# One stick-breaking pass in three steps instead of four, a small product issued later, and 70 column-square additions given to GpSimd

## The chip, the cores and the metric

The kernel runs on one core of a Trainium2 chip. A core has five engines that work at the same time, each through its own queue of instructions in a fixed order: TensorE (PE, matrix products, with its weight loads shown apart as PEld), VectorE (DVE), ScalarE (ACT), GpSimd (POOL) and SyncE (SP, which here issues transfers). They share an on-chip memory of 128 partitions. A tile of "128x512" has one row of 512 elements on each partition. An instruction that needs another engine's result waits on a semaphore, and everything behind it in the same queue waits with it.

The metric is the device time of one execution in microseconds (us). Smaller is better.

## The reference

One inference step of a two-layer decoder with D = 1024. A prompt of 1024 tokens and 8 sample tokens pass through the same weights. Cut to what matters here:

```python
def rmsnorm(x, g):
    return x * lax.rsqrt(jnp.mean(x * x, axis=-1, keepdims=True) + EPS) * g

# layer 0: HGRN2 recurrence beside attention into 256 memory tokens, then a SwiGLU FFN
# then one shared K/V is projected from the residual stream
# layer 1: stick-breaking attention over the shared K/V beside memory attention, then an FFN
h = h + rmsnorm(mix, g[1])
h = h + rmsnorm(swiglu(rmsnorm(h, g[2]), w_gu, w_down), g[3])

def stick_breaking(q, k, v, bias, ...):          # blocks of 128 queries, 4 heads
    z = q @ k.T * scale + bias
    mask = k_pos < q_pos
    log_keep = where(mask, log_sigmoid(-z), 0)
    tail = cumsum(log_keep, reverse=True) - log_keep
    w = where(mask, exp(log_sigmoid(z) + tail), 0)
    return w @ v
```

The outputs are the residual streams of prompt and sample, the recurrence states, the shared K/V and the memory K/V.

## The kernel before, in words

**Tiling.** The prompt is cut in two groups of 512 tokens, g = 0 and g = 1; group 1 carries the 8 sample tokens as well, so its tiles are 520 columns wide. Activations lie with features on the partitions, eight tiles of 128 features for D = 1024. Every f32 weight tile is split into a high and a low part, the high part by a cast on ACT (line 217 or 618), the low part by a subtraction on DVE (line 218 or 620); a product then takes three matmuls per weight tile (high times high, high times low, low times high). Lines 231, 551, 625 and 797 are those matmuls, so PE often waits, when it waits, for a weight part `ws`. A part of each FFN is computed by a scheme with fewer products (`ffn_w`, `gate_up_w`), which adds up blocks of weights first (lines 605 to 612 on DVE). Sums of weights that are used often are made ahead of time by GpSimd's accumulating transfers, "weight sums" (lines 695 to 700).

**Order of the work.** The kernel is written as Python generators. `weave` advances several of them in turn by given weights, `drain` runs one to its end. The order in which instructions are written, data dependencies and the number of buffers in each pool (four tiles `c`, seven tiles `b`, two tiles `n`) feed a scheduler that fixes each engine's queue. So a change in one generator can move instructions of its neighbours.

**Column squares.** The RMS norm needs, for every token, the sum of squares over 1024 features. `sq_acc` (lines 284 to 290) is called for eight feature tiles: the first square goes into the accumulator `st`; each of the other seven goes into a tile `n` on ACT (line 289), and DVE adds it to the accumulator (line 290). `rstd_from` then splits the accumulator in a high part (cast on ACT, line 238) and a low part (subtraction on DVE, line 239), sums over the partitions with two matmuls against ones (line 279), and takes logarithm and exponential on ACT (lines 280 and 281). The results scale the next projection's input.

**Token scales.** At the very start, `token_scales` computes the first norm's scale per token; a diagonal tile (line 363) is multiplied with ones on PE (line 368) so that every partition has all 512 scales, and ACT copies them to `rows`. `gate_proj` multiplies by them.

**Stick-breaking, group 0.** `sb_prompt` runs four heads with three units each (the blocks of queries 0 and 2 together, block 1, block 3). `weights` makes a unit's scores on PE (line 1609), adds bias and mask on DVE (lines 1620 and 1622), takes two ACT passes for softplus into a tile `e` (lines 1595 and 1596), scans on DVE (line 1632), subtracts (line 1634) and exponentiates on ACT (line 1635). `turn` transposes the result on PE (line 1641) and copies it on ACT (line 1643), `values` multiplies by the values on PE (line 1652). `step` shifts units through `asked`, `scored` and `turned`: a unit's scores are made in one step, the transposes come two steps later, the values one step after that, and three empty steps at the end flush the rest. The tile `e` is half of a `c` tile; the FFN's weight blocks (the operands `c` of lines 605 to 620) are in `c` tiles too. This pass is woven with memory attention on one side and with parts 0 and 1 of the other group's FFN on the other.

Of the kernel before, what the change touches and what calls it, by code (L numbers as in the profile page):

```python
# [23 lines left out]
def tile_decoder(  # L24
# [96 lines left out]
    def S():  # L121
        return smp.tile([P, 512], F32, tag="s", name=nm("s"))
# [149 lines left out]
    def rstd_from(acc, n, inv, dst=None, bank=NS):  # L272
# [8 lines left out]
        nc.scalar.activation(r[:, :n], r[:, :n], AF.Exp, scale=-0.5)  # L281
        return r

    def sq_acc(acc, src, k, n):
        if k == 0:
            nc.scalar.activation(acc[:, :n], src, AF.Square)
        else:
            t = N()
            nc.scalar.activation(t[:, :n], src, AF.Square)  # L289
            nc.vector.tensor_add(acc[:, :n], acc[:, :n], t[:, :n])  # L290

    def normed(g, R, rstd, gc, out, keep=False):
        n = NG[g]
# [56 lines left out]
    def token_scales(out):  # L350
        ss = small([P, 8], tag="rr")
        for tb in range(CH):
            xt = xtok[0][:, tb, :]
            junk = M().rearrange("p a n -> p (a n)")[:, :D]
            with tc.issue_after(turned[-1][tb % 2]):
                if tb % 2:
                    nc.vector.tensor_tensor_reduce(junk, xt, xt, 1.0, 0.0, ALU.mult, ALU.add, ss[:, tb : tb + 1])
                else:
                    nc.scalar.activation(junk, xt, AF.Square, accum_out=ss[:, tb : tb + 1])
        nc.scalar.activation(ss[:, :CH], ss[:, :CH], AF.Ln, scale=1.0 / D, bias=epsb)  # L360
        nc.scalar.activation(ss[:, :CH], ss[:, :CH], AF.Exp, scale=-0.5)
        d = B()
        nc.vector.tensor_mul(
            d.rearrange("p (c t) -> p c t", c=CH), ident.unsqueeze(1).to_broadcast([P, CH, P]),
            ss[:, :CH].unsqueeze(2).to_broadcast([P, CH, P]),
        )
        ps = S()
        nc.tensor.matmul(ps, ones, d, start=True, stop=True)
        rows = M()[:, 0, :G]
        nc.scalar.copy(rows, ps)  # L370
        out.extend((ss, rows))

    def start(g, out):
        if g:
# [900 lines left out]
                nc.vector.tensor_copy(vs[:, h, :], t[:, G : G + NB])  # L1275
            yield

    def gate_proj(g, W, xt, Ft, Kt, rows):
        n = NG[g]
        for h in range(H):  # L1280
            if h % 2 == 0:
                Ft.append(A())
                Kt.append(A())
            ps = proj(g, W, 0, ND, 4 * P + h * P, xt)
            f = T()
            if rows is None:
                nc.scalar.copy(sv(f, g), pv(ps, g))
            else:
                nc.vector.tensor_mul(sv(f, g), pv(ps, g), rows)
            e = T()  # L1290
            nc.vector.scalar_tensor_tensor(e[:, :n], f[:, :n], -1.0, f[:, :n], op0=ALU.mult, op1=ALU.min)
            nc.scalar.activation(e[:, :n], e[:, :n], AF.Exp)
            nc.scalar.activation(e[:, :n], e[:, :n], AF.Ln, bias=1.0)
            nc.vector.scalar_tensor_tensor(e[:, :n], f[:, :n], 0.0, e[:, :n], op0=ALU.min, op1=ALU.subtract)
            nc.vector.tensor_sub(f[:, :n], e[:, :n], f[:, :n])
            Fd = Ft[-1][:, h % 2, :n]
            Kd = Kt[-1][:, h % 2, :n]
            nc.scalar.activation(Fd, e[:, :n], AF.Exp)
# [188 lines left out]
    class mixer_a:  # L1487
# [7 lines left out]
            return lambda dst, ps, g: evac(dst, ps, g, self.scales[1])  # L1495

        def fq(self):
            yield from gate_proj(self.g, self.W, self.xt, self.F, self.K, self.scales[1])
            yield from heads2(self.g, self.W, 0, self.xt, self.scaled(silu), A, self.Q)

        def v(self):
# [96 lines left out]
    def sb_prompt(g, Qs, xo):  # L1598
# [5 lines left out]
        def weights(h, kh, unit, first):  # L1604
            ps, spans, o = S(), [], 0
            for c, s in unit:
                w = (c + 1) * P if s == g else G
                spans.append((c, s, o, w))
                nc.tensor.matmul(  # L1609
                    ps[:, o : o + w], Qs[h // 2][:, h % 2, c * P : (c + 1) * P], kh[:, s, :w], start=True, stop=True  # L1610
                )
                o += w
            zb = B()
            bh, i = biasp[:, h : h + 1], 0
            for c, s, a, w in spans:
                if s != g:
                    continue
                j = a + w - P
                if i < j:
                    nc.vector.tensor_scalar(zb[:, i:j], ps[:, i:j], bh, 44.0, op0=ALU.add, op1=ALU.min)  # L1620
                i = j + P
                nc.vector.scalar_tensor_tensor(zb[:, j:i], ps[:, j:i], bh, cap, op0=ALU.add, op1=ALU.min)
            if i < o:
                nc.vector.tensor_scalar(zb[:, i:o], ps[:, i:o], bh, 44.0, op0=ALU.add, op1=ALU.min)
            if not spare:
                c = C()
                spare.extend((c[:, 0], c[:, 1]))
            e = spare.pop(0)
            softplus(zb, e, o)
            for c, s, a, w in spans:  # L1630
                d = e[:, a : a + w][:, ::-1]
                nc.vector.tensor_tensor_scan(d, d, d, first.get(c, 0.0), op0=ALU.add, op1=ALU.max)
                first[c] = e[:, a : a + 1]
            nc.vector.tensor_sub(zb[:, :o], zb[:, :o], e[:, :o])
            nc.scalar.activation(zb[:, :o], zb[:, :o], AF.Exp)  # L1635
            return zb, spans, o
# [26 lines left out]
        def step(new=None):  # L1663
            nonlocal asked, scored, turned
            old, turned = turned, asked and (*asked[0], *turn(*asked[1]))
            asked, scored = scored, new
            if old:
                values(*old)

        for h in range(H):  # L1670
# [4 lines left out]
            for i, unit in enumerate(units):  # L1675
                step(((h, vh, i), weights(h, kh, unit, first)))
                yield
        for _ in range(3):
            step()
            yield  # L1680

# [178 lines left out]
        f0.acc = fw.acc  # L1860

    weave((chain(a1.merge(), a1.mem()), 36), (ms, 74), (rest(), 33))
    xk0, xb0 = [], []
    o1 = out_proj(1, 0, M)
    drain(o1.mm(a1.xo, 0, 1, True))
# [7 lines left out]
    b0.open(True)  # L1873
    set_banks(True)
    fw = ffn_w(1, 0, o1.x, (5, 6, 5), 0, False, beside=(0, 1), src=o1.R)
    weave((chain(b0.sb(), b0.mem()), 26), (chain(fw.part(0), fw.part(1)), 28))
    p4 = fw.part(4)
    back = b0.load()
    drain(fw.part(2), islice(back, 4))
    weave((chain(fw.part(3), islice(p4, 8)), 20), (weight_sums(1, (4,)), 16))  # L1880
    weave((p4, 4), (back, 8))
    f1 = ffn(1, 0, o1.x)
    f1.R, f1.acc = fw.R, fw.acc
# [63 lines left out]
```

## Time and profile before

| | |
|---|---|
| median of 3 runs | 2404.77 us (2404.55 to 2404.97) |
| the profiled execution | 2404.09 us |
| its span, first to last instruction | 2402.4 us |
| granted TensorE clock, mean | 0.998 |
| PE busy | 2379.4 us, 99% of the span |
| DVE busy | 1711.9 us, 71% |
| ACT busy | 1323.8 us, 55% |
| POOL busy | 113.0 us, 5% |

Lines of a view by time have a start in microseconds from the span's start, a duration, the engine, the line, the operation and the tiles (output <- inputs). Rows that follow each other closely are joined: x96 is 96 instructions, and the duration is that of all of them. A bracket at the end is the idle time of the engine just ahead of the row, and what ended it. Rows of windows give the window, its length, then for PE, PEld, DVE, ACT and POOL the busy time (and number of instructions), then the granted clock as a share of full speed, the share of DMA engines busy, and GB/s.

### The profile page before, as it was taken

The numbers are of one execution on the slowest core, as the hardware profiler recorded it, in microseconds if no ns is written. First come the engines' busy times: TensorE is split into PE (matmuls) and PEld (weight loads), VectorE is DVE, ScalarE is ACT, GpSimd is POOL, SyncE is SP. The second block draws the span as 40 slices with busy tenths as digits, with TensorE's granted clock in tenths as the row PEclk, the third lists the DMA queues.
The fourth block names the chain that finished last, engine by engine and source line by source line (L and its number), as shares of the span: only waits on it lengthen the run. The fifth ranks groups of instructions, "written<-read, shape, count | busy, mean of one in ns | idle before, by whom it ended". The sixth has DMA issues, their size and how long they took to land.

```text
span 2402.4 us, 42455 instructions
## 1 busy us (share of the span) xinstructions
PE 2379.4 (99%) x15962; PEld 2159.8 (90%) x15962; DVE 1711.9 (71%) x3197; ACT 1323.8 (55%) x2734; POOL 113.0 (5%) x187
## 2 busy tenths in 40 slices
PE   8999999999999999999999999999999999999998
PEld 7888989888889998899999989887778989999998
DVE  5867558766776676778665777876776779676866
ACT  4547544454664554566544554568547566554545
POOL 1001202101000000000001100112000000000000
PEclk9999999999999999999999999999999999999999
DMA  6354776677535446332668746544454354343442
GB/s 195 118 171 115 174 203 159 166 188 197 169 105 164 140 146 203 104 119 90 170 177 219 212 143 189 167 144 149 121 174 123 96 156 128 118 127 100 115 124 76
DMA packets 515231, 357.58 MB, mean 149 GB/s; under 512 B 20245, under 2 KB 463746, under 8 KB 515026
## 3 DMA queue, kind: packets, MB, share of 16 engines
q1 hardware_dynamic: 499154, 312.93, 43.9%
q0 software_dynamic: 15872, 41.95, 7.5%
q8 instruction: 125, 2.05, 0.4%
q14 instruction: 80, 0.66, 0.1%
HBM read 322.86 MB, written 65.49 MB: 162 GB/s over the span
## 4 chain that ended last, share of the span: by engine, by line
PE 93%; DVE 3%; ACT 2%; DMA 1%; issue 1%; SPq 0%; DVEq 0%; ACTq 0%
PE mm L231 42%; PE q L625 18%; PE q L797 12%; PE q L551 4%; PE mm L1250 2%; PE s L1429 1%; PE s L1609 1%; PE s L1652 1%; PE s L1066 1%; PE s L1047 1%; PE mm L983 1%; PE mm L1010 1%; PE q L829 1%; PE s L551 1%; PE s L1641 1%
## 5 line engine op out<-in xcount | busy, mean ns | idle before, releaser
L231 PE MATMUL mm<-x,ws 128*128 128x512 f32 (+1 forms) x5016 | 924.1, 342 | 3.7 <-ACT b L1635 1.7
L231 PEld LDWEIGHTS mm<-x,ws 128*128 128x128 f32 x5016 | 775.1, 188 | 114.5 <-ACT b L1635 2.1
L217 ACT CAST ws<-w 128x512 fp32r<-128x512 f32 x596 | 346.0, 584 | 392.9 <-PE mm L231 229.2
L218 DVE TENSOR_TENSOR ws<-w,ws 128x512 fp32r<-128x512 f32 x596 | 380.3, 645 | 222.5 <-ACT ws L217 219.0
L797 PE MATMUL q<-m,ws 128*128 128x260 f32 (+1 forms) x2496 | 304.6, 283 | 1.6 <-ACT m L238 1.0
L797 PEld LDWEIGHTS q<-m,ws 128*128 128x128 f32 x2496 | 300.1, 188 | 3.1 <-ACT m L238 1.6
L625 PE MATMUL q<-y,ws 128*128 128x260 f32 (+1 forms) x1920 | 251.0, 285 | 0.0
L625 PEld LDWEIGHTS q<-y,ws 128*128 128x128 f32 x1920 | 238.4, 189 | 2.2 <-DVE ws L620 0.7
L625 PE MATMUL q<-x,ws 128*128 128x260 f32 (+1 forms) x1668 | 220.0, 283 | 3.5 <-DVE ws L620 1.7
L625 PEld LDWEIGHTS q<-x,ws 128*128 128x128 f32 x1668 | 207.9, 189 | 4.3 <-DVE ws L620 2.1
L231 PE MATMUL mm<-m,ws 128*128 128x512 f32 x768 | 186.9, 397 | 0.0
L618 ACT CAST ws<-w 128x512 fp32r<-128x512 f32 x206 | 124.9, 619 | 97.6 <-PE q L797 30.8
L231 PEld LDWEIGHTS mm<-m,ws 128*128 128x128 f32 x768 | 142.7, 188 | 31.9
L620 DVE TENSOR_TENSOR ws<-w,ws 128x512 fp32r<-128x512 f32 x206 | 139.3, 688 | 43.6 <-ACT ws L618 40.7
L806 DVE TENSOR_TENSOR r<-r,q 128x260 f32<-128x260 f32 (+1 forms) x160 | 60.6, 420 | 49.0 <-PE q L797 48.2
L551 PE MATMUL q<-x,ws 128*128 128x260 f32 (+1 forms) x720 | 87.1, 282 | 0.0
L551 PEld LDWEIGHTS q<-x,ws 128*128 128x128 f32 x720 | 86.4, 188 | 0.3
L238 ACT CAST m<-t 128x512 fp32r<-128x512 f32 (+1 forms) x88 | 54.6, 621 | 40.3 <-DVE t L870 16.9
L618 ACT CAST ws<-b 128x512 fp32r<-128x512 f32 x82 | 50.6, 620 | 42.3 <-PE q L797 13.4
L239 DVE TENSOR_TENSOR m<-t,m 128x512 fp32r<-128x512 f32 (+1 forms) x88 | 60.8, 691 | 14.7 <-ACT m L238 13.9
L620 DVE TENSOR_TENSOR ws<-b,ws 128x512 fp32r<-128x512 f32 x82 | 56.4, 688 | 19.3 <-ACT ws L618 18.9
L290 DVE TENSOR_TENSOR st<-st,n 128x512 f32<-128x512 f32 (+1 forms) x91 | 62.3, 692 | 3.4 <-ACT n L289 1.9
(427 smaller groups left out, 3119.3 us busy)
## 6 DMA issues: line engine op xcount, KB each, us to landing
w<-in_w_gu SPq DMA_DIRECT2D x275, 256.0 KB
w<-in_w_down SPq DMA_DIRECT2D x160, 256.0 KB
wsum<-in_w_gu POOLq DMA_DIRECT2D x48, 512.0 KB, 6.6
w<-in_w_in_a SPq DMA_DIRECT2D x80, 256.0 KB
w<-in_w_o SPq DMA_DIRECT2D x64, 256.0 KB
w<-wsum SPq DMA_DIRECT2D x61, 256.0 KB
b<-in_w_gu SPq DMA_DIRECT2D x39, 256.0 KB
b<-wsum SPq DMA_DIRECT2D x39, 256.0 KB
```

The costliest lines, as they stand in the source:

```text
L217: nc.scalar.copy(ws[:, 0, :n, :], raw[:, :n, :])
L218: split[0] = nc.vector.tensor_sub(ws[:, 1, :n, :], raw[:, :n, :], ws[:, 0, :n, :].bitcast(F32))
L231: nc.tensor.matmul(ps[:, a, : PW[g]], wt, xt[k][:, xi, o : o + PW[g]], start=(k == 0 and wi == 0), stop=(k == nk - 1 and wi == 2),)
L238: nc.scalar.copy(dst[0], src)
L239: nc.vector.tensor_sub(dst[1], src, dst[0].bitcast(F32))
L290: nc.vector.tensor_add(acc[:, :n], acc[:, :n], t[:, :n])
L551: ins = nc.tensor.matmul(pp[a][:, :h], wt, xt[k][:, xi, a * h : (a + 1) * h], start=(k == 0 and wi == 0), stop=(k == ND - 1 and wi == 2),)
L618: nc.scalar.copy(w[:, 0, :], src)
L620: split[0] = nc.vector.tensor_sub(w[:, 1, :], src, w[:, 0, :].bitcast(F32))
L625: nc.tensor.matmul(ps[:, :h], w[:, wj, k * P : (k + 1) * P], x[:, xi, :], start=(first and k == 0 and wi == 0), stop=(k == 3 and wi == 2), ...
L797: nc.tensor.matmul(pp[a][:, :h], wt, mids[k][:, xi, a * h : (a + 1) * h], start=(k == 0 and wi == 0), stop=(k == nf - 1 and wi == 2),)
L806: nc.vector.tensor_add(d, d, pp[a][:, :h])
```

## The change

There are three edits. **A**: a flag `free` sends line 290's additions to GpSimd while it is set. It is set ahead of layer 0's last output projection, is taken back for the one stretch in which weight sums are being made, and is set again after that. By the order of the changed program 70 of the 91 additions move, as ten sums of seven; the remaining 21 stay on DVE. **B**: the ones product of the token scales moves from `token_scales` to a function that `gate_proj` calls at its first head. **C**: in stick-breaking of group 0, `step` passes a new unit straight on, so that the transposes come one step after the scores instead of two; two empty steps flush instead of three; `e` comes from the pool of `b` tiles; the weight in `weave` is 25 instead of 26.

```diff
+    free = [False]
     def sq_acc(acc, src, k, n):
...
-            nc.vector.tensor_add(acc[:, :n], acc[:, :n], t[:, :n])
+            (nc.gpsimd if free[0] else nc.vector).tensor_add(acc[:, :n], acc[:, :n], t[:, :n])
...
+        out.extend((ss, d))
+
+    def scale_rows(scales):
         ps = S()
-        nc.tensor.matmul(ps, ones, d, start=True, stop=True)
+        nc.tensor.matmul(ps, ones, scales[1], start=True, stop=True)
         rows = M()[:, 0, :G]
         nc.scalar.copy(rows, ps)
-        out.extend((ss, rows))
+        scales[1] = rows
...
-                nc.vector.tensor_mul(sv(f, g), pv(ps, g), rows)
+                if h == 0:
+                    scale_rows(scales)
+                nc.vector.tensor_mul(sv(f, g), pv(ps, g), scales[1])
...
-            if not spare:
+            if g and not spare:
                 c = C()
                 spare.extend((c[:, 0], c[:, 1]))
-            e = spare.pop(0)
+            e = spare.pop(0) if g else B()
...
-            asked, scored = scored, new
+            asked, scored = (scored, new) if g else (new, None)
...
-        for _ in range(3):
+        for _ in range(2 + g):
...
     weave((chain(a1.merge(), a1.mem()), 36), (ms, 74), (rest(), 33))
+    free[0] = True
...
-    weave((chain(b0.sb(), b0.mem()), 26), (chain(fw.part(0), fw.part(1)), 28))
+    weave((chain(b0.sb(), b0.mem()), 25), (chain(fw.part(0), fw.part(1)), 28))
     p4 = fw.part(4)
     back = b0.load()
     drain(fw.part(2), islice(back, 4))
+    free[0] = False
     weave((chain(fw.part(3), islice(p4, 8)), 20), (weight_sums(1, (4,)), 16))
+    free[0] = True
     weave((p4, 4), (back, 8))
```

In the changed file lines lie 2 to 8 further down: 290 is 292 there, 551 is 556, 620 is 625, 625 is 630, 643 is 648, 1609 is 1616, 1632 is 1639, 1641 is 1648.

The first place is where the FFN's part 0 ends and its part 1 begins, beside stick-breaking's first head. DVE's queue before. Tiles `b` and the scanned `c` are stick-breaking; `ws`, `n` and the `c` of lines 605, 609 and 620 are weight blocks of the FFN:

```order
L1632 SCALAR_TENSOR_TENSOR c_10786<-c_10786 128x512
L1622 SCALAR_TENSOR_TENSOR b_10942<-s_10940,biasp,cap 128x128
L1634 TENSOR_TENSOR b_10783<-b_10783,c_10786 128x512
L1632 SCALAR_TENSOR_TENSOR c_10786<-c_10786 128x128
L620 TENSOR_TENSOR ws_10808<-c_10296,ws_10808 128x512
L1632 SCALAR_TENSOR_TENSOR c_10786<-c_10786 128x384
L605 TENSOR_TENSOR n_10824<-c_10297 128x512
L1634 TENSOR_TENSOR b_10848<-b_10848,c_10786 128x512
L1632 SCALAR_TENSOR_TENSOR c_10945<-c_10945 128x256
L620 TENSOR_TENSOR ws_10826<-n_10824,ws_10826 128x512
L609 TENSOR_TENSOR c_10296<-c_10297 128x512
```

And the changed program's, the stretch of the same weight blocks (its lines 610, 614, 615 and 625 are 605, 609, 610 and 620 of before, its 569 is 564):

```order
L239 TENSOR_TENSOR m_10619<-t_10468,m_10619 128x520
L610 TENSOR_TENSOR n_10835<-c_10297 128x512
L1639 SCALAR_TENSOR_TENSOR b_10627<-b_10627 128x256
L1641 TENSOR_TENSOR b_10624<-b_10624,b_10627 128x256
L625 TENSOR_TENSOR ws_10837<-n_10835,ws_10837 128x512
L614 TENSOR_TENSOR c_10297<-c_10296,c_10297 128x512
L615 TENSOR_TENSOR c_10296<-c_10297 128x512
L569 TENSOR_SCALAR t_10708<-q_10651 128x260
L569 TENSOR_SCALAR t_10708<-q_10652 128x260
L625 TENSOR_TENSOR ws_10881<-c_10296,ws_10881 128x512
L617 TENSOR_TENSOR c_10296<-c_10296,w_10813 128x512
L542 TENSOR_TENSOR t_10640<-t_10640,t_10708 128x520
```

The weight parts of part 1's first products stood between the scans of three units; now they stand around the scan of 256 columns and ahead of the last elementwise work of part 0 (line 569, before 564). PE's queue at the same place, before:

```order
L1609 MATMUL s_10781<-a_10298,a_9838 128x512
L1641 MATMUL s_10792<-ident,b_10305 128x128 x4
L1609 MATMUL s_10845<-a_10841,a_9838 128x128
L1609 MATMUL s_10845<-a_10841,a_9838 128x384
L1641 MATMUL s_10858<-ident,b_10624 128x128 x2
L1652 MATMUL s_10863<-b_10797,a_10299 128x128 x4
L1609 MATMUL s_10940<-a_10841,a_9838 128x256
L1652 MATMUL s_10863<-b_10861,a_10299 128x128 x2
L625 MATMUL q_10804<-x_10151,ws_10808 128x260 x3
```

and now:

```order
L1616 MATMUL s_10789<-a_10298,a_9838 128x512
L1648 MATMUL s_10800<-ident,b_10624 128x128 x2
L1659 MATMUL s_10805<-b_10638,a_10299 128x128 x4
L630 MATMUL q_10815<-x_10151,ws_10819 128x260 x3
L630 MATMUL q_10815<-x_10155,ws_10819 128x260 x3
L630 MATMUL q_10815<-x_10195,ws_10819 128x260 x3
L630 MATMUL q_10815<-x_10199,ws_10819 128x260 x3
L630 MATMUL q_10816<-y_10355,ws_10837 128x260 x6
L630 MATMUL q_10816<-y_10577,ws_10837 128x260 x6
L1616 MATMUL s_10856<-a_10852,a_9838 128x128
L1616 MATMUL s_10856<-a_10852,a_9838 128x384
```

Three units' scores stood in one bunch ahead of the FFN's first product; now one unit's scores stand there, and the next unit's follow 24 matmuls later.

The second place is in layer 1, where group 0's output projection is scaled and added to the residual (lines 442 and 448) and the new residual's squares are summed, beside group 1's query projections. DVE's queue before (`st_16589` is the accumulator, `m` and `ht` are residual tiles, `ws` is a weight part of the projections):

```order
L290 TENSOR_TENSOR st_16589<-st_16589,n_16604 128x512
L448 TENSOR_TENSOR m_15463<-m_15463,ht_16591 128x512 x2
L442 SCALAR_TENSOR_TENSOR m_15464<-m_15464,par,st_15466 128x512
L290 TENSOR_TENSOR st_16589<-st_16589,n_16611 128x512
L448 TENSOR_TENSOR m_15464<-m_15464,ht_16592 128x512
L290 TENSOR_TENSOR st_16589<-st_16589,n_16677 128x512
L218 TENSOR_TENSOR ws_16694<-w_16692,ws_16694 128x512
L290 TENSOR_TENSOR st_16589<-st_16589,n_16683 128x512
L442 SCALAR_TENSOR_TENSOR m_15464<-m_15464,par,st_15466 128x512
```

and now:

```order
L453 TENSOR_TENSOR m_15469<-m_15469,ht_16597 128x512 x2
L447 SCALAR_TENSOR_TENSOR m_15470<-m_15470,par,st_15472 128x512
L218 TENSOR_TENSOR ws_16700<-w_16698,ws_16700 128x512
L453 TENSOR_TENSOR m_15470<-m_15470,ht_16598 128x512
L447 SCALAR_TENSOR_TENSOR m_15470<-m_15470,par,st_15472 128x512
```

The additions are gone from DVE's queue, and the weight part stands one residual row further ahead.

The third place is ACT's queue at the last sum, in the FFN of layer 1 (function tables are loaded where the kind of function changes; 633 to 665 are the FFN's own activations). Before:

```order
L280 ACT_TABLE_LOAD
L280 ACTIVATE st_21029<-ns_21413,epsb 128x512
L238 CAST m_21406<-t_21301 128x512
L280 ACTIVATE st_21029<-ns_21417,epsb 128x8
L637 ACTIVATE q_21350<-q_21349 128x256
L281 ACT_TABLE_LOAD
L281 ACTIVATE st_21029<-st_21029 128x520
L643 ACT_TABLE_LOAD
L643 ACTIVATE t_21462<-q_21347 128x256
```

and now (648 is 643, 670 is 665; the load for line 280 stands four rows further ahead):

```order
L280 ACTIVATE st_21035<-ns_21423,epsb 128x8
L648 ACT_TABLE_LOAD
L648 ACTIVATE t_21468<-q_21353 128x256
L281 ACT_TABLE_LOAD
L281 ACTIVATE st_21035<-st_21035 128x520
L663 COPY t_21487<-q_21354 128x256
L623 CAST ws_21555<-w_21553 128x512
L623 CAST ws_21583<-b_21581 128x512
L238 CAST x_21430<-n_21428 128x520
L638 ACTIVATE q_21516<-q_21514 128x256
L670 ACT_TABLE_LOAD
L670 ACTIVATE t_21468<-t_21489 128x256
```

An activation of the FFN now stands between lines 280 and 281, so that there are four table loads here where there were three.

More of the change, by code (lines that the diff above doesn't have):

```diff
@@ L1276, in v_proj, with gate_proj @@
             yield
-    def gate_proj(g, W, xt, Ft, Kt, rows):
+    def gate_proj(g, W, xt, Ft, Kt, scales):
         n = NG[g]
@@ L1285, in gate_proj @@
             f = T()
-            if rows is None:
+            if scales[1] is None:
                 nc.scalar.copy(sv(f, g), pv(ps, g))
             else:
-                nc.vector.tensor_mul(sv(f, g), pv(ps, g), rows)
+                if h == 0:
+                    scale_rows(scales)
+                nc.vector.tensor_mul(sv(f, g), pv(ps, g), scales[1])
             e = T()
@@ L1497, in fq @@
         def fq(self):
-            yield from gate_proj(self.g, self.W, self.xt, self.F, self.K, self.scales[1])
+            yield from gate_proj(self.g, self.W, self.xt, self.F, self.K, self.scales)
             yield from heads2(self.g, self.W, 0, self.xt, self.scaled(silu), A, self.Q)
```

## The prediction

> **What bounds the kernel now.** I read the page's totals first, then the chain that ended last, then windows for the stretches that the change touches, then rows by time inside them.
>
> ```profile
> span 2402.4 us, 42455 instructions
> PE 2379.4 (99%) x15962; PEld 2159.8 (90%) x15962; DVE 1711.9 (71%) x3197; ACT 1323.8 (55%) x2734; POOL 113.0 (5%) x187
> PE 93%; DVE 3%; ACT 2%; DMA 1%; issue 1%; SPq 0%; DVEq 0%; ACTq 0%
> L290 DVE TENSOR_TENSOR st<-st,n 128x512 f32<-128x512 f32 (+1 forms) x91 | 62.3, 692 | 3.4 <-ACT n L289 1.9
> ```
>
> PE is busy for 2379.4 of 2402.4 us: all of its idle time is 23.0 us, and the change takes no matmul away. The 70 additions that leave DVE are worth 70 x 0.69 = 48 us of DVE, but DVE is busy for 71% and no bound over the whole; that sum says nothing. What counts is the idle time of PE in the stretches that the edits touch, and time in which PE ran at a lower clock.
>
> ```profile
> 1000.00:1020.00 20.00, 18.70 (x144) 17.20 (x142) 10.27 (x23) 8.28 (x16) 0.00 (x0) 1.00 0.26 75
> 1020.00:1040.00 20.00, 18.90 (x136) 17.51 (x136) 19.52 (x36) 14.78 (x30) 0.00 (x0) 0.91 0.31 87
> 1040.00:1060.00 20.00, 18.57 (x148) 17.53 (x148) 14.94 (x35) 13.06 (x31) 0.00 (x0) 1.00 0.38 117
> 1480.00:1500.00 20.00, 18.07 (x147) 17.57 (x146) 16.54 (x27) 10.59 (x19) 0.00 (x0) 1.00 0.72 226
> 1960.00:1980.00 20.00, 19.48 (x159) 18.85 (x158) 15.74 (x28) 17.46 (x31) 0.00 (x0) 1.00 0.61 170
> ```
>
> In the first three (the first stick-breaking's beginning, edit C) PE misses 1.30, 1.10 and 1.43 us, and in the second the mean clock is 0.91. The fourth and fifth are stretches of edit A: 1.93 and 0.52 us.
>
> **Edit C, the first stick-breaking.** Where the 1.30 and 1.10 us come from, PE first, then DVE:
>
> ```profile
> 1019.75 0.51 PE L625 MATMUL q<-x,ws 128*128 128x260 f32 x2 [1.28 <-ACT ws L618]
> 1021.36 1.81 PE L625 MATMUL q<-x,ws 128*128 128x260 f32 x10 [1.10 <-DVE ws L620]
> ...
> 1018.33 1.21 DVE L1632 TENSOR_TENSOR_SCAN c<-c 128x512 f32<-128x512 f32 x1
> 1019.70 0.68 DVE L1634 TENSOR_TENSOR b<-b,c 128x512 f32<-128x512 f32 x1
> 1020.30 0.42 DVE L1632 TENSOR_TENSOR_SCAN c<-c 128x128 f32<-128x128 f32 x1
> 1020.64 0.67 DVE L620 TENSOR_TENSOR ws<-c,ws 128x512 fp32r<-128x512 f32 x1
> 1002.00:1014.00 12.00, 12.00 (x100) 11.95 (x100) 4.65 (x11) 3.70 (x7) 0.00 (x0) 1.00 0.07 21
> 1022.00:1024.00 2.00, 2.00 (x12) 2.00 (x12) 2.00 (x5) 1.21 (x3) 0.00 (x0) 0.57 0.00 0
> 1024.00:1026.00 2.00, 2.00 (x7) 1.08 (x6) 2.00 (x4) 1.11 (x3) 0.00 (x0) 0.58 0.04 8
> ```
>
> The first weight part of the FFN's part 1 (ACT line 618, DVE line 620 at 1020.64) stands on DVE behind a scan of 1.21, a subtraction of 0.68 and a scan of 0.42 us. PE has nothing else ready and stands for 1.28 and then 1.10 us, and for the next 4 us its clock is 0.57 and 0.58. The second window's mean clock of 0.91 prices that at 0.09 x 20 = 1.8 us. For the 12 us from 1002 to 1014 DVE was busy for only 4.65: there was room for the weight parts ahead of the scans. The order of the changed program uses it: these weight parts now stand around the small scan of 1004 and ahead of line 564, and three bunched units' scores are spread, 24 matmuls apart. So the two gaps should go, with the clock: 1.28 + 1.10 + 1.8 = 4.2 us. The 1.43 us of the third window is waits of line 797 for the halves `m` of part 0's and 1's results (lines 238 and 239), which the spreading may or may not shorten: I take half, 0.7.
>
> The Trainium skill ("TensorE: Matmul & The Clock Gate", "What's actually happening") puts the fall to half clock behind an idle window of about 3.4 us. The trace differs: 0.57 after gaps of 1.28 and 1.10 us. By that rule the 1.8 us would not hang on the gaps and edit C would give 1.8 less; the measurement decides.
>
> What C adds: the transposes come one step after the scores, so a unit's chain has less cover. The chain of a unit of 512 columns, in a quiet place:
>
> ```profile
> 1059.16 0.62 DVE L1620 TENSOR_SCALAR b<-s,biasp 128x384 f32<-128x384 f32 x1 [0.95 <-PE s L1609]
> ...
> 1061.07 0.64 ACT L1596 ACTIVATE c<-c 128x512 f32<-128x512 f32 x1
> 1061.75 1.23 DVE L1632 TENSOR_TENSOR_SCAN c<-c 128x512 f32<-128x512 f32 x1 [1.12 <-ACT c L1596]
> 1063.01 0.69 DVE L1634 TENSOR_TENSOR b<-b,c 128x512 f32<-128x512 f32 x1
> 1063.73 0.63 ACT L1635 ACTIVATE b<-b 128x512 f32<-128x512 f32 x1 [2.02 <-DVE b L1634]
> ```
>
> That is 1064.36 - 1059.16 = 5.2 us from scores to a matrix that can be transposed. In the changed order two of the twelve units have only some 5 us of PE work between scores and transposes (26 of the FFN's matmuls at 12.00/100 = 0.12 us and 1.8 us of stick-breaking's own), the others 6 to 16. Two units that come 0.4 us late cost 0.8. Bounds: nothing, or each of the twelve late by 0.5, 6 us. I am near the low end since ten have cover. `e` from the `b` pool costs nothing: no row of before waits for a `b` tile there, and `c` tiles come free for weight blocks; if seven `b` tiles were short, the units would run later by the same price. SP issues the next weight blocks and memory keys earlier; the DMA engines are busy for 0.26 to 0.38 there, so that hides. Sum of C: -4.2 - 0.7 + 0.8 = **-4.1**, from -4.2 - 1.4 = -5.6 to -4.9 + 6 = +1.1.
>
> **Edit A, additions on GpSimd.** The cost of one such addition on GpSimd no row shows. The nearest:
>
> ```profile
> L695 POOL COPY mk<-r 128x1 f32<-128x1 f32 x9 | 2.3, 259 | 697.0 <-DVE r L806 668.8 <-ACT r L459 28.1
> L1775 POOL TENSOR_SCALAR_AFFINE_SELECT cap<-cap 128x128 f32<-128x128 f32 x1 | 0.3, 284 | 0.0
> 364.55 0.21 POOL L695 COPY mk<-a 128x1 f32<-128x1 f32 x1 [58.04 <-ACT a L1485]
> 372.19 1.96 POOL L695 COPY mk<-a 128x1 f32<-128x1 f32 x1
> 372.22 1.29 DVE L218 TENSOR_TENSOR ws<-w,ws 128x512 fp32r<-128x512 f32 x2
> ```
>
> A select over 128 columns takes 0.28 us; four times that is 1.1 us for 512, which I take. Not below DVE's 0.69, and at most about 1.1 + 1.75 = 2.9: a copy of one element takes 0.21 us alone and 1.96 where DVE runs tensor-tensor operations back to back, 1.75 more. The Trainium skill ("GPSIMD Engine Reference", 3.1) has a two-input addition at 1.96 times DVE's time, by which it would be an estimated 1.36 us.
>
> Where it gains, in the 1480 stretch:
>
> ```profile
> 1492.42 2.67 PE L231 MATMUL mm<-x,ws 128*128 128x260 f32 x20 [0.86 <-DVE ws L218]
> 1496.17 4.09 PE L231 MATMUL mm<-x,ws 128*128 128x260 f32 x32 [1.07 <-ACT a L1485]
> 1489.88 0.69 DVE L290 TENSOR_TENSOR st<-st,n 128x512 f32<-128x512 f32 x1
> 1491.08 0.69 DVE L290 TENSOR_TENSOR st<-st,n 128x512 f32<-128x512 f32 x1
> 1491.68 0.69 DVE L218 TENSOR_TENSOR ws<-w,ws 128x512 fp32r<-128x512 f32 x1
> 1494.99 0.63 ACT L289 ACTIVATE n<-m 128x512 f32<-128x512 f32 x1 [3.10 <-DVE m L448]
> ```
>
> PE waits 0.86 us for a weight part behind these two additions on a DVE that works without a pause; without them (2 x 0.6 = 1.2 us in steps of 0.6) it is there in time. The second wait is for ACT's line 1485, which stands behind a square that waited 3.10 us for DVE's residual, late by the same additions. Both go: **-1.9** (0 if the adds only change place). In the 1960 stretch ACT is the limit, busy 17.46 of 20:
>
> ```profile
> 1975.46 1.28 ACT L281 ACT_TABLE_LOAD   x1
> 1977.41 1.28 ACT L643 ACT_TABLE_LOAD   x1
> 1979.14 1.66 PE L625 MATMUL q<-x,ws 128*128 128x256 f32 x12 [0.52 <-ACT t L643]
> ```
>
> PE already waits 0.52 us for the activation behind the second of these loads. The changed order has a fourth load, 1.28 us more on ACT; less 0.8 for weight parts that DVE makes sooner: **+0.5** (0 to +1.8). Lastly the end of each of the ten sums: the seventh addition, the split and then line 279, in PE's order among other matmuls. In the trace the split ends only 0 to 0.35 us ahead of its matmul at six of them, as here:
>
> ```profile
> 867.60 0.68 DVE L239 TENSOR_TENSOR n<-st,n 128x512 fp32r<-128x512 f32 x1
> 868.36 0.48 PE L279 MATMUL ns<-n,onesr 128*128 128x512 f32 x1
> ```
>
> The subtraction ends at 867.60 + 0.68 = 868.28, the matmul starts at 868.36. An addition of 1.1 instead of 0.69 comes 0.4 us later; six times, one quarter not hidden by the place the scheduler gave it: 6 x 0.4 x 0.25 = **+0.6** (0 to 2.4). At the other four the slack is over 1 us and hides it. GpSimd's own queue: four gathers of cached keys are passed by the first adds of layer 1; POOL is busy for 5% and is idle there, so nothing else waits. Sum of A: -1.9 + 0.5 + 0.6 = **-0.8**, from -1.9 - 0.8 = -2.7 to +13.5 (the upper end is the first rival).
>
> **Edit B, the ones product.** PE's 0.81 us of idle time sit right ahead of it:
>
> ```profile
> 35.85 1.13 PE L368 MATMUL s<-b,ones 128*128 128x512 f32 x2 [0.81 <-DVE b L363]
> ```
>
> In the code it now comes after the first gate projection, but the scheduler still issues it directly ahead of that projection's matmuls; only the transpose of line 157 (0.23 us) passes it. So the edit hardly does what it says: **-0.3**, from -0.8 to 0.
>
> **Sum.** -4.1 - 0.8 - 0.3 = -5.2 us, against 2404.09 of the profiled execution 2398.9. The median of the runs lies 0.68 above that execution, so 2399.6. The measurement can tell 0.2%, 4.8 us, from no change: this forecast lies just beyond that line.
>
> **Rivals.** *GpSimd and DVE hold each other up (slower).* The copy of 1.96 us shows GpSimd waiting for DVE. If an addition takes 1.1 us and waits 0.9 on the way, each sum's end comes 1.3 us later than DVE's 0.69: at the six sums without slack 6 x 1.3 = 7.8. If DVE's two-input operations wait for the addition as well, the 14 additions in DVE's full stretches cost it 1.1 instead of 0.69 each: 14 x 0.4 = 5.7. Together +13.5, less 4.4 for the other edits: +9.1, 2413.9. It decides slower when A costs over 9.2 us. For it speaks the copy; against it that DVE has gaps in most of these stretches, and that no row shows DVE waiting. The Trainium skill ("SBUF — State Buffer", "Who interferes with whom") says that a DVE instruction with two inputs in that memory and a GpSimd instruction that reads it exclude each other for the whole instruction; the trace agrees on GpSimd's side only. 20%.
>
> *The shorter pipeline gives its gain back (same).* Were half of the twelve units late by 0.5 us, 3.0, and half of these stops to push the weight parts behind them by as much again, 1.5, C would keep 4.9 - 4.5 = 0.4: with A and B as above -1.5, 2403.3. For it speak DVE's 19.52 of 20 us busy between 1020 and 1040; against it the spread scores. 20%.
>
> *All gaps go.* C without its cost and the third gap closed (-5.6), A's bound of -2.7, B -0.8, and 3 us from DVE's relief in other stretches: -12.1, 2392.7. 10%.
>
> *The order shifts something else that no row announces, a few us up:* 7%.
>
> **How the numbers follow.** My forecast, 43%, with a range of its own from 2394 to 2403: of it 0.28 lies beyond -4.8 us, 0.15 within. With the gains of the third rival 0.38 faster; within 0.2%: 0.15 + 0.18 + 0.03 = 0.36; slower: 0.20 + 0.02 + 0.04 = 0.26. The range runs from the third rival, 2392, to the middle of the first, 2412; about 0.15 is left out.
>
> **What would show it.** C right: no idle time over 0.5 us ahead of line 630 around 1020, granted clock 1.00 in that window; wrong: PE waits for the exponential of line 1635's counterpart at its transposes. A right: the 0.86 and 1.07 us ahead of 1492 and 1496 gone, GpSimd's additions near 1.1 us; wrong: over 2 us, or PE waiting ahead of line 279. B: an idle time still near 0.8 us ahead of the ones product. I am wrong if additions beside a full DVE stretch both engines.

## The result, and the profile after

The changed kernel takes 2438.64 us (median of 4 runs, 2434.56 to 2439.71), against 2404.87 before in the same comparison. The ratio is 1.0134, with a 95% interval of 1.0122 to 1.0146: 1.3% slower, 34 us, where the prediction said 2399.6 and 2392 to 2412. The profiled execution is the shortest of the four, 2434.56 us, so its trace shows some 4 us less loss than the median.

The page's totals of the changed kernel, and the rows of two groups:

```profile
span 2432.9 us, 42533 instructions
PE 2384.6 (98%) x15962; PEld 2161.4 (89%) x15962; DVE 1720.8 (71%) x3127; ACT 1323.9 (54%) x2735; POOL 222.6 (9%) x257
L292 POOL TENSOR_TENSOR st<-st,n 128x520 f32<-128x520 f32 (+1 forms) x70 | 110.0, 1577 | 790.2 <-ACT n L291 789.1
L218 DVE TENSOR_TENSOR ws<-w,ws 128x512 fp32r<-128x512 f32 x596 | 395.1, 671 | 220.9 <-ACT ws L217 215.5
```

PE has the same 15962 matmuls and is idle for 2432.9 - 2384.6 = 48.3 us instead of 23.0; it is also busy 5.2 us longer for the same work. DVE is the surprise: it runs 70 instructions fewer and is busy 8.9 us longer, where some 40 us fewer were to be expected (70 rows of 0.69 us are 48, but rows that follow each other overlap a little; the runs below put it at 39.5). Line 218, which nobody touched, takes 671 ns in the mean instead of 645. An addition on GpSimd takes 1.58 us in the mean.

What PE waited for, by engine, line and releaser (total, times, longest):

```profile
PE ns L279 <- ACT n L238: 12.0, 6, 5.0
PE mm L231 <- DVE ws L218: 6.1, 4, 2.8
...
PE q L630 <- ACT q L638: 2.7, 2, 2.0
PE ns L445 <- DVE m L449: 2.1, 2, 1.8
```

The first row is the end of the column-square sums, and what ACT waited for there is GpSimd:

```profile
ACT n L238 <- POOL st L292: 17.2, 10, 3.1
ACT n L291 <- POOL st L292: 10.2, 9, 2.7
```

The first stick-breaking, which lost most before, is better. The same three windows, after:

```profile
1000.00:1020.00 20.00, 20.00 (x168) 19.90 (x168) 14.64 (x29) 11.01 (x20) 0.00 (x0) 1.00 0.19 54
1020.00:1040.00 20.00, 19.48 (x155) 18.38 (x155) 14.99 (x30) 12.01 (x26) 0.00 (x0) 1.00 0.29 88
1040.00:1060.00 20.00, 19.45 (x149) 17.64 (x148) 17.99 (x37) 15.35 (x33) 0.00 (x0) 1.00 0.34 103
```

PE misses 0, 0.52 and 0.55 us instead of 1.30, 1.10 and 1.43, and the clock is 1.00 throughout. So the loss is in edit A's stretches. Here is one, by time: GpSimd's row joins three additions, and beside it stand DVE's and then PE's rows.

```profile
1497.34 5.41 POOL L292 TENSOR_TENSOR st<-st,n 128x512 f32<-128x512 f32 x3 [8.90 <-ACT n L291]
...
1496.92 1.29 DVE L453 TENSOR_TENSOR m<-m,ht 128x512 f32<-128x512 f32 x2
1498.13 1.78 DVE L447 SCALAR_TENSOR_TENSOR m<-m,par,st 128x512 f32<-128x512 f32 x1
1499.84 1.77 DVE L218 TENSOR_TENSOR ws<-w,ws 128x512 fp32r<-128x512 f32 x1
1501.53 1.77 DVE L453 TENSOR_TENSOR m<-m,ht 128x512 f32<-128x512 f32 x1
1503.22 1.40 DVE L447 SCALAR_TENSOR_TENSOR m<-m,par,st 128x512 f32<-128x512 f32 x2
...
1501.66 3.14 PE L231 MATMUL mm<-x,ws 128*128 128x260 f32 x24 [0.96 <-DVE ws L218]
1507.56 4.79 PE L231 MATMUL mm<-x,ws 128*128 128x260 f32 x25 [2.76 <-DVE ws L218]
```

Three additions on GpSimd take 5.41 us, and in the same time three DVE instructions with two inputs in on-chip memory take 1.77 us each, where a neighbour without GpSimd beside it takes 0.65 to 0.70 (1.29 and 1.40 for two). By these times the engines take turns, one instruction each: 5.41/3 = 1.80 is DVE's 0.7 and 1.1 for GpSimd. PE then waits 0.96 and 2.76 us for the weight parts that come late, in the stretch where the additions' departure was to remove 1.9.

The dearest single place is the last sum. PE, POOL, ACT and DVE by time:

```profile
2049.50 3.03 PE L556 MATMUL s<-x,ws 128*128 128x260 f32 x24
2057.58 0.80 PE L279 MATMUL ns<-n,onesr 128*128 128x512 f32 x1 [5.05 <-ACT n L238]
...
2055.34 1.54 POOL L292 TENSOR_TENSOR st<-st,n 128x512 f32<-128x512 f32 x1 [2.49 <-ACT n L291]
...
2054.56 0.63 ACT L291 ACTIVATE n<-r 128x512 f32<-128x512 f32 x1 [0.32 <-DVE r L811]
2056.91 0.62 ACT L238 CAST n<-st 128x512 fp32r<-128x512 f32 x1 [1.71 <-POOL st L292]
...
2049.00 0.42 DVE L324 TENSOR_TENSOR b<-x 128x260 f32<-128x260 f32 x1
2051.62 1.84 DVE L324 TENSOR_TENSOR b<-x 128x260 f32<-128x260 f32 x2
2053.73 0.74 DVE L811 TENSOR_TENSOR r<-r,q 128x256 f32<-128x256 f32 x2
```

And the window after the wait:

```profile
2058.00:2062.00 4.00, 4.00 (x19) 3.81 (x19) 2.90 (x8) 2.07 (x4) 0.00 (x0) 0.53 0.23 66
```

An addition of line 324 takes 0.42 us at 2049.00; at 2051.62, beside GpSimd, two take 1.84. Line 811 stands behind them, and the last square (2054.56) waits for line 811. GpSimd's last addition ends at 2056.88, the split follows, and PE, whose queue has line 279 next, stands for 5.05 us. Its clock is 0.53 for the next 4 us.

### The profile page after: what moved, and what is told of

Same layout as the page of the kernel before. It is cut to its first block, busy times and chain, and to the rows that moved or that the text cites. A ratio compares the mean times of both kernels' runs of the same rounds, so it can differ in the third digit from the quotient of the medians.

```text
span 2432.9 us, 42533 instructions
## 1 busy us (share of the span) xinstructions
PE 2384.6 (98%) x15962; PEld 2161.4 (89%) x15962; DVE 1720.8 (71%) x3127; ACT 1323.9 (54%) x2735; POOL 222.6 (9%) x257
## 5 line engine op out<-in xcount | busy, mean ns | idle before, releaser
L218 DVE TENSOR_TENSOR ws<-w,ws 128x512 fp32r<-128x512 f32 x596 | 395.1, 671 | 220.9 <-ACT ws L217 215.5
L292 POOL TENSOR_TENSOR st<-st,n 128x520 f32<-128x520 f32 (+1 forms) x70 | 110.0, 1577 | 790.2 <-ACT n L291 789.1
L625 DVE TENSOR_TENSOR ws<-w,ws 128x512 fp32r<-128x512 f32 x206 | 141.0, 696 | 47.4 <-ACT ws L623 44.0
```

What stands on the lines that cost most here:

```text
L218: split[0] = nc.vector.tensor_sub(ws[:, 1, :n, :], raw[:, :n, :], ws[:, 0, :n, :].bitcast(F32))
L292: (nc.gpsimd if free[0] else nc.vector).tensor_add(acc[:, :n], acc[:, :n], t[:, :n])
L625: split[0] = nc.vector.tensor_sub(w[:, 1, :], src, w[:, 0, :].bitcast(F32))
```

## The experiments

All times are medians; "before" in each comparison was 2404.3 to 2404.8 us. The theories: **1**, GpSimd's addition and DVE's two-input instructions exclude each other, and each addition costs by that, wherever its result goes. **2**, the addition is only longer, so the sums end late and PE waits at line 279.

**Edits B and C without A.**

```diff
-            (nc.gpsimd if free[0] else nc.vector).tensor_add(acc[:, :n], acc[:, :n], t[:, :n])
+            nc.vector.tensor_add(acc[:, :n], acc[:, :n], t[:, :n])
```

> Edits B and C without A: all 91 column-square additions on DVE as before. In the trace of the changed kernel PE's clock time runs 4.8 us ahead between 970 and 1190 us (stick-breaking) and 0.6 at the start, and loses everything elsewhere. If B and C are independent of A this gives 2404.8 - 5.4 = 2399.4 (both theories). If A's removal uncovers waits in stick-breaking, it stays near 2404.

Measured: 2400.38 us (11 runs), ratio 0.9981, interval 0.9972 to 0.9990. The rest of the change is worth 4.2 us, and A costs 2438.64 - 2400.38 = 38.3 by the medians. This kernel is better than both others. Its page beside the changed kernel's:

```profile
span 2397.4 us, 42471 instructions
PE 2377.5 (99%) x15962; PEld 2157.9 (90%) x15962; DVE 1711.0 (71%) x3197; ACT 1322.9 (55%) x2734; POOL 112.9 (5%) x187
```

The difference of the spans, 35.5 us, is 28.4 of PE's idle time and 7.1 of PE's busy time at a lower clock. Where it builds up, by the start of PE's n-th matmul in the two traces:

| in the changed kernel, us | behind the kernel without A, us |
|---|---|
| 861 | 0.0 |
| 971 | 7.9 |
| 1200 | 8.4 |
| 1435 | 14.7 |
| 1517 | 19.1 |
| 1961 | 21.1 |
| 2051 | 28.4 |
| 2065 | 35.4 |

GpSimd has additions from 847 to 963, 1366 to 1431, 1487 to 1513, 1918 to 1983 and 2032 to 2055: all but some 3 us come there or in the 10 us after.

**Edit A alone.** B and C are undone in the changed kernel (their parts of the diff, taken back):

```diff
-            asked, scored = (scored, new) if g else (new, None)
+            asked, scored = scored, new
...
-            e = spare.pop(0) if g else B()
+            e = spare.pop(0)
```

> Edit A alone. If A is the whole cause and independent: 2438.6 + 5.4 = 2444. If part of the loss came from A together with the shorter pipeline, less: 2425 to 2438.

Measured: 2440.57 us, ratio 1.0149 (1.0134 to 1.0165): 36 us slower than before by itself. Added up, 2404.6 + 38.3 = 2442.9 was to be expected; the 2.3 us between lie within the interval. A is the cause, and the edits are independent within what can be told.

**The 70 additions left out.**

```diff
-            (nc.gpsimd if free[0] else nc.vector).tensor_add(acc[:, :n], acc[:, :n], t[:, :n])
+            if not free[0]:
+                nc.vector.tensor_add(acc[:, :n], acc[:, :n], t[:, :n])
```

> Edits B and C, with the 70 additions left out altogether (the sums then hold the first square only; the norms are wrong by that). This is what a GpSimd that cost nothing and kept nobody waiting would give. Theory 1 (GpSimd and DVE exclude each other) and theory 2 (only the longer addition makes the sums late) both expect 2394 to 2399 here: whatever lies between this and the changed kernel's 2438.6 is the price of having GpSimd do it. A theory by which the new order of the queues is the cause expects 2420 or more, since the order here has no additions on DVE either.

Measured: 2397.97 us, ratio 0.9974 (0.9965 to 0.9984). Without the additions anywhere the kernel gains only 2.4 us over having them all on DVE. The intervals of the two overlap, so about 2.4 us, perhaps less, is the most that edit A could have brought with this order of the queues. The page gives the price on the other side, since DVE has the same 3127 instructions here as in the changed kernel:

```profile
PE 2378.4 (99%) x15962; PEld 2159.9 (90%) x15962; DVE 1671.5 (70%) x3127; ACT 1324.5 (55%) x2735; POOL 113.5 (5%) x187
```

DVE's 1720.8 less 1671.5 is 49.3 us: GpSimd's 70 additions stretched the other DVE instructions by more than the additions had cost on DVE (1711.0 less 1671.5, 39.5 us, by the page of the kernel without A).

**The last addition of each sum back on DVE.**

```diff
-            (nc.gpsimd if free[0] else nc.vector).tensor_add(acc[:, :n], acc[:, :n], t[:, :n])
+            (nc.gpsimd if free[0] and k < ND - 1 else nc.vector).tensor_add(acc[:, :n], acc[:, :n], t[:, :n])
```

> The changed kernel with the seventh addition of each of the ten sums on DVE, the other 60 on GpSimd. Theory 2 (lateness of the sum's end): the 12.6 us that PE waits ahead of line 279 go nearly all, with what the clock loses after them, 2420. Theory 1 (exclusion): DVE's stretched operations stay, the gain is only the last addition's 0.9 us at ten places and what hangs on it, 2430 to 2436.

Measured: 2432.46 us, ratio 1.0110 (1.0094 to 1.0125). Six of the 38 us go, as theory 1 had it. The wait at line 279 halves (its row below, beside 12.0 in the changed kernel), but the waits for weight parts stay:

```profile
PE ns L279 <- ACT n L238: 6.7, 4, 3.7
PE mm L231 <- DVE ws L218: 6.1, 4, 2.7
```

**Idle additions on GpSimd beside DVE's.** All additions are on DVE, and GpSimd adds the tile of squares to itself, for nobody:

```diff
+            nc.vector.tensor_add(acc[:, :n], acc[:, :n], t[:, :n])
+            if free[0]:
+                nc.gpsimd.tensor_add(t[:, :n], t[:, :n], t[:, :n])
```

> Edits B and C with all 91 additions on DVE, and in the places of the 70 GpSimd additions a GpSimd addition of the tile of squares to itself, behind DVE's, whose result nobody uses. No sum ends later by GpSimd's own time; only what GpSimd's addition does to its neighbours is left. Theory 1 (exclusion): DVE's two-input operations beside it are stretched as in the changed kernel (there by some 52 us in all), and DVE has 48 us of its own additions beside that: 2420 to 2440. Theory 2 (lateness): 2400 to 2404, as without A.

Measured: 2436.94 us, ratio 1.0130 (1.0114 to 1.0147): 36.6 us over the kernel without them, for results that nobody reads. Not all of that is exclusion: ACT waited 20.1 us for tiles `n` that GpSimd still held, which makes sums late too.

**Constants written by GpSimd in the same places.**

```diff
+            if free[0]:
+                nc.gpsimd.memset(t[:, :n], 1.0)
```

> The same as the kernel with the twin additions, but GpSimd fills the tile with a constant: it writes the same tile at the same place in its queue and reads nothing. If exclusion needs a GpSimd instruction that reads on-chip memory, 2400 to 2403 and no stretched DVE operations; if any GpSimd access excludes DVE, about as the twin additions.

Measured: 2400.33 us, ratio 0.9983 (0.9974 to 0.9993), the same as without them. The group of fills:

```profile
L294 POOL MEMSET n<- 128x520 f32 (+1 forms) x70 | 37.1, 530 | 834.6 <-DVE st L292 604.0 <-PE mm L231 230.0
```

One of them by time, with DVE's rows beside it, in a stretch as dense as the one above:

```profile
1488.48 0.52 POOL L294 MEMSET n<- 128x512 f32 x1 [0.62 <-DVE st L292]
...
1488.34 0.68 DVE L218 TENSOR_TENSOR ws<-w,ws 128x512 fp32r<-128x512 f32 x1
1488.94 0.68 DVE L292 TENSOR_TENSOR st<-st,n 128x512 f32<-128x512 f32 x1
```

DVE's two-input subtraction takes its usual 0.68 us with GpSimd writing beside it. And it is not that the fills are shorter: they run for 37.1 us in all, and DVE's busy time is 1710.7 us, against 1711.0 in the kernel without them. What excludes DVE here is a GpSimd instruction that reads. This pair is the decisive one: the same engine, the same places in the queue, the same tile. (Whether reading one tile would do as reading two was not tried.)

**Idle additions that hold no tile.** GpSimd reads the feature tile that is squared and writes a small tile of its own, 400 columns, so nothing waits for its result or its input:

```diff
+    junk = const.tile([P, 400], mybir.dt.bfloat16, name="junk")
...
+            if free[0]:
+                nc.gpsimd.tensor_add(junk, src[:, :400], src[:, :400])
```

> As the twin additions (all 91 additions on DVE, 70 idle ones on GpSimd), but GpSimd's reads the feature tile that is being squared and writes a tile of its own (400 columns in place of 512 to 520, for want of room), so that no tile of squares is held for it and nothing waits for its result. Holding `n` was a wait of its own in the twin additions (ACT waited 20.1 us for it). Theory 1 (exclusion): still dear; with 400/512 of the lock's length and without the holding, 2415 to 2430. Theory 2b (the loss comes from tiles and results that GpSimd holds longer, not from the ports): 2400 to 2404.

Measured: 2429.04 us, ratio 1.0097 (1.0081 to 1.0112): 28.7 us over the kernel without them, with 1.26 us per addition and no waiting for these additions by anyone. The waits of PE are the same two as in the changed kernel:

```profile
PE ns L279 <- ACT n L238: 8.8, 5, 3.5
PE mm L231 <- DVE ws L218: 8.5, 3, 3.5
```

Theory 2b (tiles and results that GpSimd holds longer) falls: three quarters of the loss come with nobody using the results, though these additions are shorter. And the wait at line 279, which looks like lateness of GpSimd's sum, is mostly DVE's: its stretched instructions make the squares' inputs late.

**The sums later, without GpSimd.** All additions on DVE; each of the ten sums ends with one ACT copy of the accumulator onto itself:

```diff
+            if free[0] and k == ND - 1:
+                nc.scalar.copy(acc[:, :n], acc[:, :n])
```

> Edits B and C with all additions on DVE, and the end of each of the ten sums made later by one ACT copy of the accumulator onto itself (0.6 us), with GpSimd out of it. Theory 2: ten late sums cost by themselves, in proportion 12 or more: 2412. Theory 1: lateness of this size is worth at most the 6 x 0.4 that slack does not cover: 2400 to 2404.

Measured: 2401.35 us, ratio 0.9984 (0.9975 to 0.9994), 1.0 us over the kernel without A. Ten sums that end 0.6 us later cost 1 us together (here the scheduler knows of the copies and orders PE's queue with them; a lateness that it does not know of could cost more). Theory 2 falls.

**Only the five sums of the residual, and only the five of projection results, on GpSimd.** The flag is taken back around the other calls, in the first kernel around three calls and in the second around this one:

```diff
+                free[0], was = False, free[0]
                 sq_acc(acc, R[k][:, :n], k, n)
+                free[0] = was
```

> The changed kernel with only five of the ten sums on GpSimd: those of the residual after a norm (line 457 of the changed file), where DVE works without a pause. Theory 1 expects most of the loss here, since DVE has no gaps to take the stretched operations in: 2418 to 2428. Theory 2 expects half: five sums of ten, 2416 to 2422, with the waits of line 279 as the cause.

> The changed kernel with the other five sums on GpSimd: those of projection results as they leave PE. If the price is per addition, wherever it stands, the loss of the changed kernel less that of the residual sums: 2400.4 + (38.2 - 19.6) = 2419. If the place matters: 2408 to 2414, since DVE has more gaps there.

Measured: 2419.99 us, ratio 1.0059 (1.0043 to 1.0076), and 2418.12 us, ratio 1.0058 (1.0043 to 1.0074). That is 19.6 and 17.7 us over the kernel without A, together 37.3 of 38.3. The price is about 0.5 us per addition, and in time the places hardly differ: I had expected most of it where DVE works without a pause, and that was wrong. The pages, first of the one, then of the other:

```profile
PE 2384.2 (99%) x15962; PEld 2162.9 (89%) x15962; DVE 1717.5 (71%) x3162; ACT 1323.7 (55%) x2735; POOL 170.9 (7%) x222
PE 2382.6 (99%) x15962; PEld 2161.4 (89%) x15962; DVE 1706.4 (71%) x3162; ACT 1322.8 (55%) x2734; POOL 169.6 (7%) x222
```

With the same number of instructions DVE is busy 11.1 us longer beside the sums of the residual, and yet these cost only 1.9 us more. So the time lost does not go by how much of DVE is held up.

**The two halves of edit C.** First the other pool for `e` with the four-step pipeline, then the shorter pipeline with `e` in `c` tiles (both with B, without A):

```diff
-            asked, scored = (scored, new) if g else (new, None)
+            asked, scored = scored, new
...
-        for _ in range(2 + g):
+        for _ in range(3):
```

> Of edit C only the other pool for `e` (and the weight 25), with the pipeline of four steps and with edit B; A left out. In this kernel's queue order the weight parts stand ahead of the scan of 512 columns, as with all of C. If the freed `c` tiles are what lets the weight blocks come early: 2400 to 2401, as with B and C. If it is the shorter pipeline: 2404.

```diff
-            if g and not spare:
+            if not spare:
...
-            e = spare.pop(0) if g else B()
+            e = spare.pop(0)
```

> Of edit C only the shorter pipeline (and the weight 25), with `e` in halves of `c` tiles as before and with edit B; A left out. If the freed `c` tiles are the cause: 2403 to 2405, both gaps still there. If the shorter pipeline is: 2400.

Measured: 2403.32 us, ratio 0.9995 (0.9986 to 1.0004), and 2405.05 us, ratio 1.0000 (0.9991 to 1.0009). Neither half shows a gain that can be told from none; both together gave 4.2. The first lies between the 2400 to 2401 and the 2404 that the two explanations expected, so the time alone decides nothing. The windows around the first two gaps say why, first of the kernel with the other pool, where the gaps are gone, then of the one with the shorter pipeline, where they are not:

```profile
1000.00:1020.00 20.00, 20.00 (x161) 19.10 (x160) 14.53 (x28) 10.45 (x20) 0.00 (x0) 1.00 0.18 54
1020.00:1040.00 20.00, 19.81 (x154) 18.36 (x154) 18.80 (x39) 15.79 (x34) 0.00 (x0) 1.00 0.32 99
```

```profile
1000.00:1020.00 20.00, 17.52 (x135) 16.28 (x133) 10.31 (x22) 8.74 (x16) 0.00 (x0) 0.97 0.26 76
1020.00:1040.00 20.00, 19.80 (x138) 18.65 (x138) 16.86 (x33) 12.87 (x27) 0.00 (x0) 0.86 0.27 84
```

So the freed `c` tiles close the gaps. The kernel with the other pool alone gives the gain back later, where the pass ends with its longer flush:

```profile
1180.00:1200.00 20.00, 16.65 (x127) 15.37 (x126) 12.43 (x23) 13.94 (x27) 0.00 (x0) 1.00 0.93 244
```

PE misses 3.35 us in that window. By PE's n-th matmul this kernel is 5.8 us ahead of before at 1054 and 1.0 at 1195. Why exactly the four-step flush makes PE wait there was not tried further.

## Why the prediction was wrong, point by point

**Edit A, additions on GpSimd, is the step that failed**: -0.8 forecast, +38.3 measured. Four of its terms, by their names there:

- *The cost of one addition.* Forecast at 1.1 us; 24 of the 70 take 1.3, and the mean is 1.58 us. Off, but not the cause: the experiment with late ends shows how little such lateness is worth.
- *The 1480 stretch, -1.9.* With the additions left out its gain does come: PE is 2.3 us further ahead there than the kernel without A. With the additions on GpSimd it loses 4.4 us instead; PE's waits of 0.96 and 2.76 us above stand there.
- *The 1960 stretch, +0.5.* The fourth table load is there (1985.28, 1992.55, 1995.52, 1997.22 and 2001.27 are five loads of 1.28 us, where the kernel without A has four). It is dearer than forecast: the kernel without additions has it too, and between PE's 12540th and 12720th matmul it takes 27.3 us where the kernel without A takes 23.4. Whether the load alone does that was not tried. (A's lower bound of -2.7 took 0.8 us off here without the load, below the 0 that was given as this term's own lower end; nothing hung on it.)
- *The ends of the ten sums, +0.6.* PE waits 12.0 us ahead of line 279, 6 times. The bound of 2.4 was for the addition's own length; what made the ends late was mostly DVE, stretched ahead of them.

What the sum left at nothing is the term that decides: DVE's other instructions beside GpSimd's, 49.3 us longer in all. The first rival named this mechanism, and it is what happened. It was sized at +13.5 for A and 2413.9 and given 20%. Its size failed in one step: DVE's waiting was counted as DVE time, for the 14 additions in its full stretches, 5.7 us net. DVE's busy time did rise by no more than 9.8 us net (1720.8 against 1711.0), but the time lost is four times that, and both kinds of places lose about 0.5 us per addition, however much of DVE they hold up. PE's waits say where it goes: 12.0 us at line 279 (the rival had 7.8), 6.1 at line 218, many smaller ones, and 7.1 us of lower clock, for which the rival had no term. It is likely, though no run sorts it out, that an addition beside a DVE with gaps still hits the instruction that PE waits for next. The sign that the prediction gave for being wrong, additions that stretch both engines beside a full DVE, is what the rows show. The argument against this rival, that no row showed DVE waiting, was no evidence: before the change GpSimd's instructions that read were mostly copies of one column, too short to hold DVE for long. The 1.96 us of such a copy showed one side of the exclusion, and the other side was the one that mattered. The rule quoted beside the rival, from the Trainium skill ("SBUF — State Buffer", "Who interferes with whom"), agrees with these runs where they test it: two inputs on DVE's side, a reading instruction on GpSimd's, the whole instruction long. Two DVE rows beside one addition show the first point:

```profile
945.49 1.64 POOL L292 TENSOR_TENSOR st<-st,n 128x520 f32<-128x520 f32 x1 [10.21 <-ACT n L291]
945.88 0.68 DVE L449 TENSOR_TENSOR m<-m,ns 128x512 f32<-128x512 f32 x1
946.47 0.68 DVE L451 TENSOR_TENSOR m<-m,xsraw 128x8 f32<-128x8 f32 x1
```

Line 449, with one input from the accumulators of PE, keeps its 0.68 us for 512 columns. Line 451, with both inputs in on-chip memory, takes as long for 8 columns, where the kernel without A has 0.16: it ends only when the addition has ended. Two inputs are not always needed, though: a copy of line 1101, with one input and 16 columns, took 1.25 us beside the addition of 1512.97, and 0.17 in the kernel without A.

```profile
1513.23 1.25 DVE L1101 COPY ss<-a 128x16 f32<-128x16 f32 x1
```

**Edit C came out at the size forecast, by another half of it than was credited**: -4.1 forecast and -0.3 for B, -4.2 for both together in the runs. The two gaps of 1.28 and 1.10 us and the clock are gone, the third window's 1.43 fell to 0.53 in the kernel without A (forecast: half), and the shorter cover cost what was said, in that kernel as in the changed one:

```profile
PE s L1648 <- ACT b L1642: 0.9, 2, 0.5
```

Two waits at the transposes, 0.9 us together, against "two units 0.4 us late". What the forecast did not see is which half does it: it credited the earlier weight parts to the spread of the units, while the experiments give the gaps to the freed `c` tiles and leave the shorter pipeline to keep that gain at the end. The remark that "`e` from the `b` pool costs nothing" was thus the main point of the edit.

The clock at the gaps went as the trace of before had it and not by the idle window of the Trainium skill ("TensorE: Matmul & The Clock Gate", "What's actually happening"), which the prediction weighed against it: with gaps of 1.28 and 1.10 us the clock fell, without them it stayed at 1.00.

**Edit B fits**: -0.3 forecast, though no run has it alone. The idle time ahead of the ones product fell from 0.81 to 0.49, with the transpose of line 157 ahead of it, not the "still near 0.8" that was named as its sign:

```profile
35.17 1.13 PE L373 MATMUL s<-b,ones 128*128 128x512 f32 x2 [0.49 <-DVE b L365]
```

## What to carry to other kernels

Work on GpSimd that reads on-chip memory is not free beside a busy DVE: each such instruction can hold a DVE instruction with two inputs there for as long as it runs. Do not price it by GpSimd's idle share, nor by DVE's busy time alone (here 9.8 us more, against 38 lost): ask which DVE result PE waits for next. Set against it what the relief of DVE can bring at most, which a run without the work tells (here 2.4 us against 38). A wait that names GpSimd's result can still be DVE's lateness; an idle copy of the work, whose result nobody uses, tells the two apart.

## What the hardware showed that I had not expected

- With both queues full, DVE and GpSimd take turns instruction by instruction: three additions in 5.41 us on GpSimd, 1.78, 1.77 and 1.77 us for the three DVE instructions beside them.
- GpSimd's fills of the same tiles (70 of 0.53 us, writing only) changed neither DVE's durations nor the time: 2400.33 against 2400.38 us.
- PE's clock fell to 0.53 for 4 us after the one gap of 5.05 us, and to 0.60 from 1508 to 1512 after that of 2.76. Over the kernel, the same 15962 matmuls took 7.1 us more of busy time, a fifth of the loss, with a mean clock of 0.997 instead of 0.999.
